# Stage 1 of a hybrid encoder kernel: x two tiles ahead, and another order of tables, value weights and value products

## The chip, the cores and the metric

The kernel runs on one core of a Trainium2 chip. The metric is the device time of one execution in microseconds (us). The engines are named as the profile names them: PE (TensorE, matmuls and transposes; its weight loads are PEld), DVE (VectorE), ACT (ScalarE), POOL (GpSimd) and SP (SyncE, which here only issues DMAs). Each engine takes its instructions in one fixed order.

## The reference

One encoder layer is applied to two groups of tokens (2048 and 512, model width 1024), with the same weights:

```python
xn = rms_norm(h, mix_norm)
z = xn @ w_in                      # 1024 x 2848
(a_q, a_k, a_v, a_gate, l_q, l_k, l_v, l_gate, lr_f, lr_b) = jnp.split(z, idx, axis=-1)
q = apply_axial_rope(rms_norm(a_q per head, q_norm), tables)
k = apply_axial_rope(rms_norm(a_k per head, k_norm), tables)
o_attn = block_attention(q, k, v)                   # 8 query heads, 2 key heads
o_gla = rms_norm(o_fwd + o_bwd, gla_norm)           # gated linear attention, both directions
h = h + concat[o_attn * silu(a_gate), o_gla * silu(l_gate)] @ w_out
gate = sigmoid(rms_norm(h, ple_norm) @ w_ple_gate)
return h + gate * (p @ w_ple_proj)                  # then a final rms_norm
```

## The kernel before

The work is staged: stage 1 (lines 111 to 343) normalises x and makes the projections that attention and the linear attention's values need; stage 2 is the linear attention, stage 3 the attention and the gates, stage 4 the output. Stages hand over through scratch tensors in HBM. Every fp32 matmul product is made from a high and a low part of both operands (`mm3`, line 101: three matmuls for each k of 128).

Stage 1 runs over 20 tiles of 128 tokens. For each tile `prep` loads the next x, takes the square sum on ACT, the power and the product `xn` on POOL (`x_r`, `xn`), transposes `xn` on PE (8 transposes into two PSUM tiles `pt`), copies the high part `xt` on ACT (line 203), makes the low part on DVE (line 204), and stores both. `project` makes three products of 24 matmuls each, into PSUM tiles `pm` (four banks): the queries with the weights `wq` (512 columns), keys, values and low-rank codes with `wm` (288), and the low-rank values with `wl` (512). After the first two come `rope` (square sums of the heads, the products with the cosine table `cqk` and the sine table `sqk`, into `rot` and `swp`), then on POOL the sum of the two, the power `h_r` of the heads' square sums and the product with it; that is called the rotation below. `post` transposes the result of the tile before and stores it. The xn tile has one buffer, x has two.

Ahead of the loop stand, in program order: 32 warm-up transposes of the identity, `prep(0)`, the weights `wq`, the load of x(1), the weights `wm` with the 32 low-rank columns `wlr`, the weights `wl`, the scale of the values (`value_scale`: squares, two small PE products, two powers on POOL), and the rope tables (loads of `ctab`, `stab` and of the head norms `qn`; two `cqk` products and eight `sqk` products, all on DVE). Each weight of 1024 rows is eight loads, eight casts on ACT (`*_h`, line 99) and eight differences on DVE (`*_l`, line 100). In the loop, tile t+1 is prepared before tile t is projected, and tile t-1 is posted after it:

```python
            nxt = prep(t + 1) if t + 1 < NT else None
            cur = project(t, xt)
            if pend is not None:
                post(t - 1, *pend)
            pend, xt = cur, nxt
```

The order in each engine's queue is not the program's. A scheduler writes it when the kernel is built: whenever an engine comes free in its own estimate of the run, it takes, of the instructions whose inputs and buffers it estimates to be ready, the first in program order. `high_priority(n)` ranks what is traced under it n places further ahead; `issue_after(e)` puts what is traced under it behind `e` on e's engine, without waiting for e to finish. Semaphores keep the run right whatever the estimate was; where the chip is late, the engine stands.

Of the kernel before, what the change touches and what calls it, by code (L numbers as in the profile page):

```python
# [9 lines left out]
F32 = mybir.dt.float32  # L10
F32R = mybir.dt.float32r
F16 = mybir.dt.float16
BF16 = mybir.dt.bfloat16
U32 = mybir.dt.uint32
AF = mybir.ActivationFunctionType
# [5 lines left out]
P = 128  # L21
# [30 lines left out]
class Net:  # L52
# [49 lines left out]
    def mm3(self, out, lh, ll, rh, rl, first=True, last=True):  # L102
        pairs = ((lh, rh), (ll, rh), (lh, rl))
        n = len(lh) * 3
        i = 0
        for k in range(len(lh)):
            for a, b in pairs:
                self.nc.tensor.matmul(out, lhsT=a[k], rhs=b[k], start=first and i == 0, stop=last and i == n - 1)  # L108
                i += 1


def stage1(net, s, gw=None):
    nc, tc, d = net.nc, net.tc, net.d
    with ExitStack() as ctx:
# [15 lines left out]
        def load_x(t):  # L130
            src = xs[0][t * P:(t + 1) * P] if t < 16 else xs[1][(t - 16) * P:(t - 15) * P]
            x = xp.tile([P, 1024], F32, name="x", tag="x")
            nc.sync.dma_start(out=x, in_=src)
            return x
# [37 lines left out]
        def part(w, c0, c1):  # L172
            return lambda k: w[:, k, c0:c1]
# [9 lines left out]
            for j in range(2):  # L183
                nc.sync.dma_start(out=s["wg"][i % 2][:, :, j, k].rearrange("j p e -> p j e"), in_=f(hl[:, j]))

        def prep(t):
            c, tt = t // 4, (t % 4) * P
            x = xq.pop(0)
            if 0 < t < NT - 1:
                xq.append(load_x(t + 1))  # L190
            ssq = net.sm.tile([P, 1], F32, name="x_ssq")
            xn = xp.tile([P, 1024], F32, name="xn", bufs=1)
            nc.scalar.activation(xn, x, AF.Square, accum_out=ssq)
            r = net.rstd(ssq, 1024.0, 1, "x")
            nc.gpsimd.tensor_scalar(xn, x, r, 1.0, ALU.mult, ALU.mult)
            xt = xp.tile([P, 2, 8, P], F32R, name="xt", bufs=2)
            for half in range(2):
                pt = ps_t.tile([P, 4, P], F32, name="pt")
                for k in range(4):
                    kk = half * 4 + k  # L200
                    nc.tensor.transpose(pt[:, k], xn[:, kk * P:(kk + 1) * P], net.ident)
                sl = slice(half * 4, half * 4 + 4)
                nc.scalar.copy(xt[:, 0, sl], pt)  # L203
                nc.vector.tensor_tensor(xt[:, 1, sl], pt, f(xt[:, 0, sl]), ALU.subtract)
            nc.sync.dma_start(out=s["xt"][c][:, :, :, tt:tt + P], in_=f(xt))
            return xt

        def project(t, xt):
# [3 lines left out]

            def proj(w, n):
                ps = ps_m.tile([P, 512], F32, name="pm")[:, :n]
                net.mm3(ps, lh, ll, [w[0][:, k] for k in range(8)], [w[1][:, k] for k in range(8)])
                return ps

            hs = net.sm.tile([P, 10], F32, name="hs")
# [30 lines left out]
            hr = net.rstd(hs, 64.0, 10, "h")  # L249
            nc.gpsimd.tensor_tensor(rot, rot, swp, ALU.add)  # L250
            nc.gpsimd.tensor_tensor(rot, rot, hr.unsqueeze(2).broadcast_to([P, 10, 64]), ALU.mult)
            pl = proj(wl, 512)
            lv = tp.tile([P, 512], F32, name="lv")
            nc.scalar.copy(lv, pl)
            nc.sync.dma_start(out=s["lv"][t // 4][t % 4], in_=lv)
            return rot.rearrange("p h e -> p (h e)"), lrin

        def post(t, rf, lrin):
            c, tt = t // 4, (t % 4) * P
# [18 lines left out]
            nc.sync.dma_start(out=s["lr"][c][:, tt:tt + P], in_=f(lr))  # L278

        warm = ps_q.tile([P, 4, P], F32, name="pqt")  # L280
        for i in range(32):
            nc.tensor.transpose(warm[:, i % 4], net.ident, net.ident)
        xt = prep(0)
        first = stage if gw is None else gw.stage
        net.weight(first, part(wq[0], 0, 512), part(wq[1], 0, 512), win, COL_Q, 512, mix)
        xq.append(load_x(1))
# [3 lines left out]
        nc.vector.tensor_tensor(w, w, mix.unsqueeze(2).broadcast_to([P, 8, 32]), ALU.mult)  # L290
        nc.scalar.copy(wm[0][:, :, 256:288], w)
        nc.vector.tensor_tensor(wm[1][:, :, 256:288], w, f(wm[0][:, :, 256:288]), ALU.subtract)
        net.weight(first, part(wl[0], 0, 512), part(wl[1], 0, 512), win, COL_LV, 512, mix)

        vscale = [value_scale()]

        ctab, stab = (gp.tile([P, 1024], F32, name=n, tag="wghl").rearrange("p (t e) -> p t e", t=16)
                      for n in ("ctab", "stab"))
        nc.sync.dma_start(out=ctab, in_=d["rope_c"])
# [19 lines left out]
        for w in range(2):  # L319
            nc.vector.tensor_tensor(cqk[:, :, w], ctab, qn[:, w:w + 1, :].broadcast_to([P, 16, 64]), ALU.mult)  # L320
            sv = sqk[:, :, w].rearrange("p t (a b e) -> p t a b e", a=2, b=2)
            tv = stab.rearrange("p t (a b e) -> p t a b e", a=2, b=2)
            for b in range(2):
                for a in range(2):
                    nc.vector.tensor_tensor(
                        sv[:, :, a, b], tv[:, :, a, b],
                        qns[:, w, a, 1 - b].unsqueeze(1).broadcast_to([P, 16, 16]), ALU.mult)

        pend = None
        for t in range(NT):  # L330
            if t >= 2 and t < 18:
                gate_weight(t - 2)
                if gw is not None and t % 2 == 0:
                    gw.main(stage, mix, t // 2 - 1, t // 2)
                if gw is not None and t == 17:
                    gw.small(tp)
            nxt = prep(t + 1) if t + 1 < NT else None
            cur = project(t, xt)
            if pend is not None:
                post(t - 1, *pend)  # L340
            pend, xt = cur, nxt
# [853 lines left out]
```

## Time and profile before

| | us |
|---|---|
| median of 3 runs | 2087.77 (2084.49 to 2088.56) |
| the profiled execution | 2088.21 |
| span of its trace | 2086.5 |
| PE busy | 2004.7 (96%) |
| DVE busy | 1332.6 (64%) |
| ACT busy | 1181.5 (57%) |
| POOL busy | 356.5 (17%) |

Stage 1 takes about the first 340 us of the span. PE's busy time says when a matmul was in it, not at which clock; the granted clock has a row of its own. The rows below come from the first 64 us of that execution and from one later tile; the POOL groups of rows 8 count the whole stage or execution. In rows that are listed in order of time, a group "x8" of equal instructions runs from the start given for the length given, and the brackets give how long the engine had been idle before it and what ended the wait.

### The profile page before, as it was taken

How to read it: one execution, taken by the hardware profiler on the slowest of the kernel's cores; microseconds unless marked ns; L12 is line 12 of the kernel's file. 1: busy time of each engine (PE TensorE's matmuls, PEld its weight loads, DVE VectorE, ACT ScalarE, POOL GpSimd, SP SyncE). 2: the span in 40 equal slices, each digit the busy share in tenths (PEclk: the TensorE clock that was granted, in tenths of full speed). 3: DMA queues.
4: the chain of work that ended last, by engine and by line, in shares of the span. 5: the costliest groups of instructions: out<-in, count | busy, mean ns of one | idle time of the engine just before them, and what ended most of it. 6: DMA issues, size and time to landing. Idle time of an engine off the chain costs nothing.

```text
span 2086.5 us, 29717 instructions
## 1 busy us (share of the span) xinstructions
PE 2004.7 (96%) x11174; PEld 1321.1 (63%) x11174; DVE 1332.6 (64%) x2242; ACT 1181.5 (57%) x2048; POOL 356.5 (17%) x292
## 2 busy tenths in 40 slices
PE   8999999999979999999999999999989999999998
PEld 7788887777754444444444444444437888888886
DVE  7555444665678889899889989988874222222223
ACT  5343233555558888788878878878883222222222
POOL 2434431000430011011011011100120111111111
PEclk9999999999999999999999999999999999999999
DMA  8887445666775225333333422522236222222220
GB/s 269 241 254 209 134 128 167 202 203 199 227 229 188 79 97 171 106 112 108 114 112 128 143 80 94 177 68 93 80 115 187 86 86 86 86 86 86 81 66 33
DMA packets 251360, 282.23 MB, mean 135 GB/s; under 512 B 41872, under 2 KB 180976, under 8 KB 246096
## 3 DMA queue, kind: packets, MB, share of 16 engines
q1 hardware_dynamic: 251072, 279.80, 43.0%
q8 instruction: 88, 1.44, 0.3%
q0 software_dynamic: 144, 0.52, 0.1%
q14 instruction: 56, 0.46, 0.1%
HBM read 189.64 MB, written 90.64 MB: 134 GB/s over the span
## 4 chain that ended last, share of the span: by engine, by line
PE 79%; DVE 8%; ACT 7%; DMA 3%; issue 2%; POOL 1%; SPq 0%; DVEq 0%; POOLq 0%; ACTq 0%
PE pm L108 38%; PE pg L728 9%; PE po L805 5%; PE px L762 4%; PE pss L816 4%; PE pss L817 4%; ACT p L818 3%; PE po L797 3%; PE pp L108 3%; PE pz L801 2%; DVE plo L827 2%; DVE mx L768 2%; ACT phi L825 2%; PE pn L845 1%; PE pt L1080 1%
## 5 line engine op out<-in xcount | busy, mean ns | idle before, releaser
L818 ACT ACTIVATE p<-pss,lnp,qk_scale 128x512 f32<-128x512 f32 x544 | 407.3, 781 | 113.4 <-PE pss L817 100.9
L768 DVE TENSOR_REDUCE mx<-px 128x1 f32<-128x512 f32 x544 | 357.0, 682 | 68.1 <-PE px L762 66.6
L728 PE MATMUL pg<-xt,wg 128*128 128x512 f32 x960 | 376.4, 484 | 1.1 <-DVE g L733 0.9
L827 DVE TENSOR_TENSOR plo<-p,phi 128x1024 f16<-128x1024 f32 x272 | 338.9, 1248 | 34.6 <-ACT phi L825 32.8
L825 ACT CAST phi<-p 128x1024 f16<-128x1024 f32 x270 | 283.2, 1049 | 5.6 <-PE po L805 0.9
L728 PEld LDWEIGHTS pg<-xt,wg 128*128 128x128 f32 x960 | 181.7, 190 | 69.1 <-issue 6.7
L816 PE MATMUL pss<-qa,ka 128*128 128x512 f16 x544 | 208.8, 385 | 11.1 <-ACT p L818 10.2
L762 PE MATMUL px<-ka,qa 128*128 128x512 f16 x544 | 201.0, 384 | 10.3 <-DVE mx L768 6.3
L817 PE MATMUL pss<-qb,kb 66*128 66x512 f16 x544 | 206.4, 383 | 0.3 <-ACT qb L781 0.3
L1128 DVE SCALAR_TENSOR_TENSOR th<-th,pp 128x512 f32<-128x512 f32 (+1 forms) x41 | 27.7, 675 | 190.0 <-ACT th L1127 190.0
L805 PE MATMUL po<-phi,v 128*128 128x512 f16 x544 | 142.5, 385 | 0.0
L108 PE MATMUL pm<-xt,wlqk 128*128 128x512 f32 x480 | 120.4, 410 | 7.8 <-DMA xt<-scr_xt 6.3
L816 PEld LDWEIGHTS <-ka 128*128 128x128 f16 x544 | 52.8, 97 | 107.0 <-issue 83.7
L1081 ACT CAST hT<-pt 128x512 fp32r<-128x512 f32 x40 | 23.5, 587 | 169.7 <-PE pt L1080 169.7
L108 PEld LDWEIGHTS pm<-xt,wlqk 128*128 128x128 f32 x480 | 94.3, 199 | 30.0 <-DMA xt<-scr_xt 7.5
L108 PE MATMUL pm<-wq_h,xt 128*128 128x512 f32 x320 | 103.2, 403 | 4.5 <-ACT xt L203 4.3
L762 PEld LDWEIGHTS <-qa 128*128 128x128 f16 x544 | 52.4, 98 | 83.9 <-issue 41.9
L1127 ACT ACTIVATE th<-pm,rh 128x512 f32<-128x512 f32 (+1 forms) x41 | 27.9, 680 | 133.8 <-PE pm L108 133.8
L108 PE MATMUL pm<-wpg0h,hT 128*128 128x512 f32 x320 | 101.0, 396 | 0.1
L108 PE MATMUL pm<-wo0h,mx 128*128 128x512 f32 x320 | 100.5, 395 | 0.0
L108 PE MATMUL pm<-wo1h,mx 128*128 128x512 f32 x320 | 100.4, 394 | 0.0
L851 POOL TENSOR_TENSOR ou<-ou,rs 128x512 f32<-128x512 f32 x20 | 35.5, 1777 | 378.5 <-DVE rs L849 378.5
(250 smaller groups left out, 3866.1 us busy)
## 6 DMA issues: line engine op xcount, KB each, us to landing
wg<-scr_wg SPq DMA_DIRECT2D x40, 1024.0 KB
scr_xt<-xt SPq DMA_DIRECT2D x20, 1024.0 KB
xt<-scr_xt SPq DMA_DIRECT2D x20, 1024.0 KB
xt<-scr_xt SPq DMA_DIRECT2D x40, 512.0 KB
scr_mx<-hl SPq DMA_DIRECT2D x40, 512.0 KB
mx<-scr_mx SPq DMA_DIRECT2D x20, 1024.0 KB
x<-x_prompt SPq DMA_DIRECT2D x27, 512.0 KB
scr_wg<-wghl SPq DMA_DIRECT2D x32, 256.0 KB
```

Of the source, the lines that this page charges most:

```text
L108: self.nc.tensor.matmul(out, lhsT=a[k], rhs=b[k], start=first and i == 0, stop=last and i == n - 1)
L728: nc.tensor.matmul(ps, lhsT=w[:, wi, k], rhs=xi, start=i == 0, stop=i == 23)
L762: nc.tensor.matmul(ps, lhsT=q[0][:, b * P:(b + 1) * P], rhs=ks[ti][0][:, h // 4], start=True, stop=True)
L768: nc.vector.tensor_reduce(mx[:, b, i:i + 1], product(i, b), axis=AX.X, op=ALU.max)
L797: nc.tensor.matmul(po[r:r + 32], lhsT=ks[t // 4][2][:, t % 4 + i, kv, g * 32:g * 32 + 32], rhs=lo[:, i], start=t == 2, stop=False)
L801: nc.tensor.matmul(pz[i * 32:i * 32 + 32], lhsT=ones, rhs=(lo, hi)[i // 2][:, i % 2], start=t == 2, stop=t + 4 == n)
L805: e = nc.tensor.matmul(po, lhsT=ks[t // 4][2][:, t % 4 + i, kv], rhs=hi[:, i], start=False, stop=t + i + 1 == n)
L816: nc.tensor.matmul(ps, lhsT=ka[:, kv, cs], rhs=q[0], start=True, stop=False)
L817: nc.tensor.matmul(ps, lhsT=kb[0:66, kv, cs], rhs=q[1][0:66], start=False, stop=True)
L818: e = nc.scalar.activation(p[:, i], ps, AF.Exp, bias=net.lnp, scale=net.qk_scale)
L825: nc.scalar.copy(hi, p)
L827: nc.vector.tensor_tensor(lo, p, hi, ALU.subtract)
```

## The change

- **x.** `prep` is cut in two. `norm(t)` takes x, its square sum (the square itself now goes to a bf16 tile of its own), the power and `xn`, and loads x(t+2); it is called two tiles ahead, and `xn` has two buffers. `prep(t, xn)` keeps the transposes, the copies and the store.
- **Start.** 40 warm-up transposes at rank 200; `prep(0)` at rank 100, its PE part behind the last warm-up.
- **Order.** The rope tables come before the weights `wl`, and x(2) is loaded between them. The eight `sqk` products move from DVE to POOL.
- **Products.** `project` stops before the value product. For tiles 0 and 1 the order of the products is q(0), k(0), preparation of tile 1 behind q(0)'s last matmul on PE, q(1), k(1), value(0), then preparation of tile 2, value(1). From tile 2 on the order in a tile is as before, with `norm(t + 2)` called between k and value.

```diff
         for k in range(len(lh)):
             for a, b in pairs:
-                self.nc.tensor.matmul(out, lhsT=a[k], rhs=b[k], start=first and i == 0, stop=last and i == n - 1)
+                e = self.nc.tensor.matmul(out, lhsT=a[k], rhs=b[k], start=first and i == 0, stop=last and i == n - 1)
                 i += 1
+        return e
...
-        def prep(t):
-            c, tt = t // 4, (t % 4) * P
+        def norm(t):
             x = xq.pop(0)
-            if 0 < t < NT - 1:
-                xq.append(load_x(t + 1))
             ssq = net.sm.tile([P, 1], F32, name="x_ssq")
-            xn = xp.tile([P, 1024], F32, name="xn", bufs=1)
-            nc.scalar.activation(xn, x, AF.Square, accum_out=ssq)
+            xn = xp.tile([P, 1024], F32, name="xn", bufs=2)
+            sq = xp.tile([P, 1024], BF16, name="xsq", bufs=1)
+            nc.scalar.activation(sq, x, AF.Square, accum_out=ssq)
             r = net.rstd(ssq, 1024.0, 1, "x")
             nc.gpsimd.tensor_scalar(xn, x, r, 1.0, ALU.mult, ALU.mult)
+            if 0 < t < NT - 2:
+                xq.append(load_x(t + 2))
+            return xn
+
+        def prep(t, xn):
+            c, tt = t // 4, (t % 4) * P
             xt = xp.tile([P, 2, 8, P], F32R, name="xt", bufs=2)
...
-                net.mm3(ps, lh, ll, [w[0][:, k] for k in range(8)], [w[1][:, k] for k in range(8)])
+                ends.append(net.mm3(ps, lh, ll, [w[0][:, k] for k in range(8)], [w[1][:, k] for k in range(8)]))
                 return ps
...
+            yield
             pl = proj(wl, 512)
             lv = tp.tile([P, 512], F32, name="lv")
             nc.scalar.copy(lv, pl)
             nc.sync.dma_start(out=s["lv"][t // 4][t % 4], in_=lv)
-            return rot.rearrange("p h e -> p (h e)"), lrin
+            yield rot.rearrange("p h e -> p (h e)"), lrin
...
         warm = ps_q.tile([P, 4, P], F32, name="pqt")
-        for i in range(32):
-            nc.tensor.transpose(warm[:, i % 4], net.ident, net.ident)
-        xt = prep(0)
+        with tc.high_priority(200):
+            for i in range(40):
+                e = nc.tensor.transpose(warm[:, i % 4], net.ident, net.ident)
+        xn = norm(0)
+        with tc.high_priority(100), tc.issue_after(e.ins):
+            xt = prep(0, xn)
...
-        net.weight(first, part(wl[0], 0, 512), part(wl[1], 0, 512), win, COL_LV, 512, mix)
-
         vscale = [value_scale()]
-
...
-                    nc.vector.tensor_tensor(
+                    nc.gpsimd.tensor_tensor(
                         sv[:, :, a, b], tv[:, :, a, b],
                         qns[:, w, a, 1 - b].unsqueeze(1).broadcast_to([P, 16, 16]), ALU.mult)
-
-        pend = None
+        xq.append(load_x(2))
+        net.weight(first, part(wl[0], 0, 512), part(wl[1], 0, 512), win, COL_LV, 512, mix)
+
+        pend, ends = None, []
+        xn = norm(1)
...
-            nxt = prep(t + 1) if t + 1 < NT else None
-            cur = project(t, xt)
+            if t == 0:
+                gen = project(0, xt)
+                next(gen)
+                with tc.issue_after(ends[0].ins):
+                    nxt = prep(1, xn)
+                early = project(1, nxt)
+                next(early)
+            else:
+                nxt = prep(t + 1, xn) if t + 1 < NT else None
+                gen = early if t == 1 else project(t, xt)
+                if t > 1:
+                    next(gen)
+            xn = norm(t + 2) if t + 2 < NT else None
+            cur = next(gen)
```

## Rows read from the trace of the kernel before

**Rows 1.** Busy time by engine in one tile's stretch; columns as in its head.

```profile
core 0: us, PE busy (x) PEld busy (x) DVE busy (x) ACT busy (x) POOL busy (x), PEclk, DMA share, GB/s
246.50:262.17 15.67, 15.67 (x87) 13.67 (x87) 7.19 (x19) 4.92 (x13) 6.48 (x5) 1.00 0.53 147
```

**Rows 2.** PE's waits to 420 us: for whom, us in total, times, longest.

```profile
PE pt L201 <- POOL xn L195: 6.8, 2, 4.7
PE pm L108 <- ACT xt L203: 4.3, 1, 4.3
```

**Rows 3.** PE in order of time: start us, length us, what [idle before, releaser].

```profile
1.43 5.53 PE L282 MATMUL pqt<-ident 128*128 128x128 f32 x32 [1.43 <-POOL ident masks.py:199]
...
14.41 0.79 PE L108 MATMUL pm<-wq_h,xt 128*128 128x512 f32 x1 [4.30 <-ACT xt L203]
...
29.61 0.63 PE L108 MATMUL pm<-wl_h,xt 128*128 128x512 f32 x2
...
35.10 0.61 PE L108 MATMUL pm<-wq_h,xt 128*128 128x512 f32 x2
...
40.54 0.42 PE L108 MATMUL pm<-wm_h,xt 128*128 128x288 f32 x2
...
46.05 1.03 PE L201 MATMUL pt<-ident,xn 128*128 128x128 f32 x8
46.84 0.48 PE L108 MATMUL pm<-wl_h,xt 128*128 128x512 f32 x1
...
56.57 1.97 PE L201 MATMUL pt<-ident,xn 128*128 128x128 f32 x8 [4.71 <-POOL xn L195]
...
63.59 0.42 PE L108 MATMUL pm<-wm_h,xt 128*128 128x288 f32 x2
```

**Rows 4.** Half microseconds, columns as in rows 1: the clock rises in them.

```profile
18.50:19.00 0.50, 0.50 (x3) 0.37 (x2) 0.32 (x2) 0.50 (x2) 0.33 (x1) 0.65 1.01 290
59.50:60.00 0.50, 0.50 (x3) 0.36 (x3) 0.39 (x1) 0.50 (x1) 0.00 (x0) 0.69 0.00 0
```

**Rows 5.** POOL in order of time.

```profile
40.52 1.57 POOL L250 TENSOR_TENSOR rot<-rot,swp 128x640 f32<-128x640 f32 x1 [5.88 <-DVE swp L233]
...
48.94 1.56 POOL L250 TENSOR_TENSOR rot<-rot,swp 128x640 f32<-128x640 f32 x1 [3.56 <-DVE swp L233]
50.61 2.40 POOL L80 TENSOR_TENSOR h_r<-h_ms,mhalf 128x10 f32<-128x10 f32 x1
...
55.40 1.12 POOL L195 TENSOR_SCALAR xn<-x,x_r 128x1024 f32<-128x1024 f32 x1
```

**Rows 6.** DVE in order of time.

```profile
18.76 0.42 DVE L292 TENSOR_TENSOR wm_l<-wlr,wm_h 128x256 fp32r<-128x256 f32 x1 [0.18 <-ACT wm_h L291]
...
27.03 4.06 DVE L100 SCALAR_TENSOR_TENSOR wl_l<-wst,mixn,wl_h 128x512 fp32r<-128x512 f32 x6
...
33.61 1.22 DVE L320 TENSOR_TENSOR cqk<-ctab,qn 128x1024 f32<-128x1024 f32 x1
...
37.30 1.42 DVE L325 TENSOR_TENSOR sqk<-stab,qn 128x256 f32<-128x256 f32 x4
...
39.24 0.74 DVE L233 TENSOR_TENSOR swp<-pm,sqk 128x256 f32<-128x256 f32 x2
```

**Rows 7.** ACT in order of time.

```profile
12.58 1.30 ACT L99 ACTIVATE wm_h<-wst,mixn 128x256 fp32r<-128x256 f32 x3 [0.96 <-DMA wst<-w_in]
13.79 1.05 ACT L203 CAST xt<-pt 128x512 fp32r<-128x512 f32 x2
...
31.96 0.30 ACT L306 ACTIVATE qabs<-qn 128x128 f32<-128x128 f32 x1
```

**Rows 8.** POOL's elementwise groups; mean ns of one behind the comma.

```profile
L250 POOL TENSOR_TENSOR rot<-rot,swp 128x640 f32<-128x640 f32 x20 | 31.3, 1567 | 98.9 <-DVE swp L233 78.3 <-DVE lrin L242 20.6
L851 POOL TENSOR_TENSOR ou<-ou,rs 128x512 f32<-128x512 f32 x20 | 35.5, 1777 | 378.5 <-DVE rs L849 378.5
```

**Rows 9.** SP's queue in order of time: the norms' load.

```profile
26.07 0.33 SPq L302 DMA_DIRECT2D qn<-q_norm  x1
```

## The prediction

> **What bounds the kernel now.** I read the list of TensorE's (PE's) waits first, then the stretches of single tiles, then the queues of each engine in time order over the first 75 us. The profiled execution took 2088.21 us, of which the trace spans 2086.5; the median of the runs is 2087.77. My sum is made against the first and lowered by their distance, 0.44 us.
>
> Stage 1 (to about 340 us) is bound by PE: one whole tile takes 15.67 us, and PE is busy for all of it [rows 1]. Twenty such tiles are the same work after the change, so only what PE loses at the start of stage 1 is in play. The waits show two losses: 6.8 us for POOL's `xn` in two waits, of which one is 4.7, and 4.3 us for ACT's `xt` [rows 2]. In PE's queue [rows 3] the first matmul starts at 14.41 after 4.30 us of waiting, and from 51.87 (the wait of 4.71 is in the row) nothing runs until 56.57.
>
> The granted clock adds to both. [...]
>
> **Why PE waits at 51.87.** It is the transposing of tile 3 that waits. POOL's queue [rows 5] shows tile 3's `xn` behind the head rotation of tile 1: `rot` at 48.94, the power for the head norms at 50.61 (2.40 us), then `xn` only at 55.40. Tile 1's rotation was late because DVE made the rope tables late: the low-rank value weights `wl_l` until 31.09, the first `cqk` product at 33.61, the last four `sqk` products until 38.72, and only then rope of tile 0 [rows 6].
>
> **The change, part by part.**
>
> *Normalising two tiles early.* `xn` of tile 3 is now asked for during tile 1's value product, a tile ahead of its transposes, and has its own second buffer. The 4.71 us of waiting (51.87 to 56.57 [rows 3]) go. With them goes the slow clock behind: from 56.57 to 63.59 PE does 8 transposes and 21 matmuls in 7.02 us. At full clock the transposes take 0.79 (46.05 to 46.84) and a matmul of this kind 0.227 (24 of them from 35.10 to 40.54 [rows 3]), so 0.79 + 4.77 = 5.56. That is 1.46 us more. What stands next in line is PE itself.
>
> *Norm work itself.* The square (now to a bf16 tile), the power and the product are the same instructions at the same count. The loads of x come one tile sooner on SP's queue and on the same buffers; x(2) becomes 0.5 MB ahead of the value weights. I cost these at nothing; PE's work on tiles 0 and 1 hides them.
>
> *Warm-up of 40, tile 0 ahead.* In ACT's queue the two `xt` copies of tile 0 stand behind three `wm_h` casts, which themselves waited for their loads until 12.58 [rows 7]. That is why PE waits 4.3 us. A higher rank decides only between instructions that the scheduler estimates to be ready; tile 0's preparation came ahead of all weights in program order before too, and lost its place all the same, so its estimated readiness was the reason. Eight more warm-up transposes ahead of it can only move that estimate back. Eight at 0.173 us (5.53 for 32 [rows 3]) are 1.4 us, at most three casts of 0.43 more; none, if the estimate hangs on `xn`. Between 14.41 and 15.7, then; I take two casts, a first matmul at 15.27. PE runs at half clock in that time, so 0.86 us late are 0.43 us of full-clock work. Cost: 0.4 us. The other end, copies right behind the transposes, is a rival below.
>
> *Tables ahead of the value weights; `sqk` to POOL.* DVE gives up 8 products of 0.36 us (2.84 for 8). No row has them on POOL. By POOL's 1567 ns for 128x640 one of 128x256 costs 0.63, by its 1777 ns for 128x512 0.89 [rows 8]: 5.0 to 7.1 us for 8. I take 0.63, whose row is in this stage, so 5.0. POOL had been idle for 5.88 us when the rotation of tile 0 began at 40.52 [rows 5], and the first user is rope of tile 0. [...]
>
> *New order of products.* Before, the four `pm` banks of PSUM held q(0), k(0), value(0), q(1), and k(1) at 40.54 needed the bank of q(0), which rope freed at 39.98 [rows 3, 6]. Now they hold q(0), k(0), q(1), k(1), and value(0) needs it. q(0), k(0) and the second preparation ended at 29.61 before [rows 3]; 0.43 later, plus 5.44 and 3.19 for q(1) and k(1), is 38.7. Is rope of tile 0 done by then? The norms' load `qn` is issued at 26.07, behind the value-scale chain [rows 9], and ACT took it up at 31.96 [rows 7]. From there it took 1.65 us to the first cosine product and 0.74 for the swap [rows 6]. With four or eight `sqk` ahead: 31.96 + 1.65 + 2.5 (or 5.0) + 0.74 = 36.9 to 39.4, and up to 4 us sooner if ACT takes `qn` up when it lands. Cost: zero, with ends of 0 and 2.8 us (eight at 0.89 give 41.5 against 38.7). The value weights' second halves take DVE 0.68 us apiece (6 in 4.06 [rows 6]), and value(0) uses one in 0.68 (three matmuls); with a start ahead of 38.7 they keep up. Cost: nothing.
>
> **Sum.** 4.71 + 1.46 - 0.43 = 5.7 us. 2088.21 - 5.7 = 2082.5; against the median 2082.0. Its own range is 2079.5 to 2083.5.
>
> **Rivals.**
>
> *1. The start moves forward.* If the copies of tile 0 stand right behind its transposes, the first matmul comes up to 4.30 us sooner. But k(0) needs the last part of `wm_l`, done at 19.18 [rows 6], and q(0) doesn't last that long; PE stands before k(0) and may lose its clock again. From 19.18 on it still has k(0) (3.19), tile 1 (15.67), value(0) (5.44) and some 2 us of small products: 45.5, or 47 with the loss of clock, against 50.7 for the same point before (three matmuls ahead of the wait). That is 3.7 to 5.2 on top of 4.71 + 1.46: 2078 to 2076.4, likeliest 2078. For it: the rank and the edge are aimed there. Against: the readiness argument.
>
> *2. value(0) waits for its bank.* As worked out, 1 to 2.8 us, or more if `qn` lands behind x(2) (0.5 MB at 290 GB/s is 1.8 [rows 4]): 2083.5 to 2086.5, likeliest 2085.
>
> *3. The change doesn't do what it says.* `xn` of tile 3 stays behind both rotations. If POOL ends `sqk` at 39.4, two tiles' POOL work (48.94 to 55.40 is 6.46 for one) and the `xn` (1.12 [rows 5]) end at 53.4, where PE wants it near 51; that is half of the old wait, and any DVE delay between brings back the rest. Against: `xn` of tile 3 has its input long before, and POOL is idle ahead of the tables. 2085 to 2088, likeliest 2087.
>
> *4. Slower: the value weights come late.* Their loads now stand behind the tables, x(2) and, at worst, behind two waits in SP's queue (the stores of `xt`, and `qn` [rows 9]). PE would stop before value(0) at 38.7, and every us counts, with about 1.5 for the clock from some 4 us on. It ends slower than before once the first cast comes after 43, and measurably so after 47. For that the loads would have to be issued after 40, behind tile 1's stores; nothing in the queue before points that far. 2090 to 2094.
>
> **How the numbers follow.** Forecast 0.50, rival 1 0.17, rival 2 0.16, rival 3 0.10, rival 4 0.07. The likeliest gives 2082. The range takes in rival 1 down to 2076 and rival 2 and most of rival 3 up to 2087.5. A measurement of this kernel tells about 0.2% (4.2 us) from no change; the forecast lies 1.6 us past that line, and the runs themselves spread by 4 us, so a fifth of it counts as no change. Faster: 0.40 + 0.17 + 0.04 = 0.61; slower 0.07 and a little for spread, 0.08; same 0.31.
>
> **What would show it.** In PE's waits the 4.7 us for `xn` must be gone, and no half clock between 20 us and the end of stage 1. ACT's `xt` copies of tile 0 behind three to six `wm_h` casts, first matmul at 14.4 to 15.7: right; copies before any `wm_h` cast: rival 1. A wait of `pm` for DVE's `swp` near 38: rival 2; for `wl_h` or `wl_l`: rival 4. The last matmul of stage 1 must come some 6 us sooner, and the stages behind must take what they took; if they do not, the sum has missed a place.

## The result: slower

| | before | after |
|---|---|---|
| median, us | 2086.03 (6 runs, 2084.49 to 2088.56) | 2096.97 (6 runs, 2093.67 to 2101.47) |
| profiled execution, us | 2088.21 | 2094.54 |
| its span, us | 2086.5 | 2092.8 |
| end of stage 1 in it, us | 340.18 | 353.22 |

Three more runs of the kernel before lower its median from 2087.77. The ratio is 1.0052, with an interval of 1.0037 to 1.0067: about 11 us slower, clear of noise though only half a per cent, where 2082.0 and a range of 2076.0 to 2087.5 were forecast. The end of stage 1 is read from the start of the last tile's transposes of `rot`, first in the kernel before, then in the changed one (start us, length us, what, idle before and its releaser):

```profile
340.18 0.63 PE L263 MATMUL pqt<-ident,rot 128*128 128x128 f32 x4 [1.32 <-DVE qt L268]
...
353.22 0.63 PE L269 MATMUL pqt<-ident,rot 128*128 128x128 f32 x4 [1.32 <-DVE qt L274]
```

So stage 1 takes 13.04 us more. PE's waits to 330 us in the changed kernel, the longest four (for whom: us in total, times, longest):

```profile
PE pm L108 <- DVE swp L238: 12.5, 1, 12.5
PE pm L108 <- ACT xt L208: 5.7, 2, 5.5
PE pt L206 <- POOL xn L194: 1.6, 1, 1.6
PE pm L108 <- DVE xt L209: 1.5, 2, 0.8
...
```

Against [rows 2]: `xn` gives back 5.2 us, 4.7 of them for tile 3, as was meant, and 0.5 for tile 0, whose transposes now come after a longer warm-up. The high half of `xt` costs 1.4 more, 1.15 for tile 0 (5.45 after 4.30) and the rest for tile 1; the low half, which had cost 0.2, costs 1.3 more. A new wait of 12.5 us for `swp` takes the place of everything gained. That is 10.0 us more. Of the other 3.0, 0.7 are the longer warm-up (6.21 us in PE's queue below, 5.53 before). The rest is mostly slow clock: PE's busy time at half clock (granted clock 0.50), counted half, comes to 5.9 us after and 3.7 before, 2.1 more; 0.2 us stay unexplained. Three stretches show the waits and the clock (length, PE busy and its matmuls, granted clock, DMA share, GB/s), first before, then after:

```profile
14.00:31.00 17.00, 16.02 (x88) 0.86 0.92 289
31.00:48.00 17.00, 17.00 (x90) 1.00 0.75 213
48.00:65.00 17.00, 12.29 (x60) 0.90 0.75 217
```

```profile
14.00:31.00 17.00, 14.25 (x74) 0.77 0.62 177
31.00:48.00 17.00, 3.78 (x16) 0.63 0.65 216
48.00:65.00 17.00, 16.68 (x78) 0.86 0.71 221
```

In the middle stretch PE has almost no work (3.78 us), and the clock falls to half: it is 0.50 from 36.0 to 52.5, and 1.00 again from 53.0. PE in order of time, to be held against [rows 3]:

```profile
1.43 6.21 PE L289 MATMUL pqt<-ident 128*128 128x128 f32 x40 [1.43 <-POOL ident masks.py:199]
...
15.77 0.79 PE L108 MATMUL pm<-wq_h,xt 128*128 128x512 f32 x1 [5.45 <-ACT xt L208]
...
31.06 1.03 PE L206 MATMUL pt<-ident,xn 128*128 128x128 f32 x8
32.37 0.50 PE L108 MATMUL pm<-wq_h,xt 128*128 128x512 f32 x1 [0.27 <-ACT xt L208]
32.71 0.29 PE L108 MATMUL pm<-wm_h,xt 128*128 128x288 f32 x1
45.51 1.19 PE L108 MATMUL pm<-wl_h,xt 128*128 128x512 f32 x2 [12.50 <-DVE swp L238]
...
48.32 0.80 PE L108 MATMUL pm<-wq_h,xt 128*128 128x512 f32 x1 [0.76 <-DVE xt L209]
```

q(0) and k(0) are followed by tile 1's transposes, by one matmul each of q(1) and k(1), and then, at 33.0, by the first matmul of value(0). It needs the bank of q(0), and rope of tile 0 frees that only at 45.4. Who holds it up stands in the queues of DVE, POOL, SP and ACT, one after the other ([rows 5, 6, 7, 9] show the same before):

```profile
32.84 1.77 DVE L326 TENSOR_TENSOR cqk<-ctab,qn 128x1024 f32<-128x1024 f32 x1
...
36.87 7.83 DVE L100 SCALAR_TENSOR_TENSOR wl_l<-wst,mixn,wl_h 128x512 fp32r<-128x512 f32 x8
44.62 0.74 DVE L238 TENSOR_TENSOR swp<-pm,sqk 128x256 f32<-128x256 f32 x2
...
47.59 0.68 DVE L209 TENSOR_TENSOR xt<-pt,xt 128x512 fp32r<-128x512 f32 x1
```

```profile
32.77 9.39 POOL L331 TENSOR_TENSOR sqk<-stab,qn 128x256 f32<-128x256 f32 x8 [7.01 <-DVE qn L319]
```

```profile
26.18 0.33 SPq L308 DMA_DIRECT2D qn<-q_norm  x1
...
27.50 5.50 SPq L97 DMA_DIRECT2D wst<-w_in  x8
```

```profile
31.37 0.31 ACT L312 ACTIVATE qabs<-qn 128x128 f32<-128x128 f32 x1 [2.56 <-DMA qn<-k_norm]
...
33.74 5.07 ACT L99 ACTIVATE wl_h<-wst,mixn 128x512 fp32r<-128x512 f32 x8
```

Read from SP on: the load of `qn` still goes out at 26.18, where [rows 9] had it at 26.07, since its buffer, shared with the tiles of the value-scale chain, waits for that chain. The eight loads of the value weights now stand behind it and go out from 27.50 to 33.0. Their first halves are cast on ACT until 38.8, their second halves fill DVE's queue from 36.87 to 44.70, and the swap of tile 0, which frees the bank, stands behind all eight. The low half of tile 1's `xt`, needed for q(1), comes later still. So PE has neither q(1) nor value(0).

### The profile page after: what moved, and what is told of

Its sections match the earlier page's. It is cut to its first block, busy times and chain, and to the rows that moved or that the text cites. A ratio compares the mean times of both kernels' runs of the same rounds, so it can differ in the third digit from the quotient of the medians.

```text
span 2092.8 us, 29710 instructions
## 1 busy us (share of the span) xinstructions
PE 2004.0 (96%) x11182; PEld 1322.1 (63%) x11182; DVE 1334.4 (64%) x2234; ACT 1180.4 (56%) x2048; POOL 365.2 (17%) x300
## 4 chain that ended last, share of the span: by engine, by line
PE 78%; DVE 8%; ACT 7%; DMA 3%; issue 3%; POOL 1%; SPq 0%; DVEq 0%; POOLq 0%; ACTq 0%
PE pm L108 38%; PE pg L749 8%; PE po L826 5%; PE px L783 4%; PE pss L837 4%; PE pss L838 4%; ACT p L839 3%; PE po L818 3%; PE pp L108 3%; DVE plo L848 2%; PE pz L822 2%; DVE mx L789 2%; ACT phi L846 2%; PE pn L866 1%; PE pt L1101 1%
## 5 line engine op out<-in xcount | busy, mean ns | idle before, releaser
L108 PE MATMUL pm<-xt,wlqk 128*128 128x512 f32 x480 | 115.6, 399 | 2.5 <-ACT l L474 1.7
L108 PE MATMUL pm<-wl_h,xt 128*128 128x512 f32 x320 | 100.1, 393 | 12.5 <-DVE swp L238 12.5
L783 PEld LDWEIGHTS <-qa 128*128 128x128 f16 x544 | 52.5, 98 | 83.6 <-issue 41.7
L872 POOL TENSOR_TENSOR ou<-ou,rs 128x512 f32<-128x512 f32 x20 | 35.5, 1775 | 378.6 <-DVE rs L870 378.6
```

The costliest lines, as they stand in the source:

```text
L108: e = self.nc.tensor.matmul(out, lhsT=a[k], rhs=b[k], start=first and i == 0, stop=last and i == n - 1)
L783: nc.tensor.matmul(ps, lhsT=q[0][:, b * P:(b + 1) * P], rhs=ks[ti][0][:, h // 4], start=True, stop=True)
```

## The experiments

Each timed kernel is given by its ratio to the kernel before on the same chip, with the interval. The theory: value(0) now hangs on rope of tile 0, which hangs on value weights that were put behind `qn`; the early norms themselves gain. (The letters A, B and C in the expectations are each run's own.) Its rivals: the products on POOL are the cause; the new order of products alone is the cause; or the whole change gains and stage 2 loses.

### Parts of the change undone

**Tile 1's preparation traced first.** The loop's edge goes, too:

```diff
-                gen = project(0, xt)
-                next(gen)
-                with tc.issue_after(ends[0].ins):
-                    nxt = prep(1, xn)
+                nxt = prep(1, xn)
+                gen = project(0, xt)
+                next(gen)
```

> The changed kernel, with the preparation of tile 1 traced ahead of q(0) again (no edge behind q(0)). Theory A (the moved preparation): in the changed kernel DVE makes the low half of tile 1's xt only at 47.6 to 49.1, behind the eight wl_l and rope of tile 0, so PE has no q(1) and k(1) to do while it waits 12.5 us for the bank of q(0). Here PE does them first (8.6 us), the wait for swp falls from 12.5 to about 4, the last matmul of stage 1 comes 8 to 10 us sooner, and the time is 2086 to 2090. Theory B (the sqk products on POOL are the cause): the bank comes free at the same time, near 45; the wait falls by the same 8.6, so the same time. Theory C (the loss is the value product's place): the wait stays above 8 us, 2093 to 2097.

Measured: 2089.28 us median of 12, ratio 1.0008 [0.9992, 1.0023]. Stage 1 ends at 348.21, 5.0 us sooner than in the changed kernel, and PE's wait for `swp` falls to 5.12 us, at 49.24:

```profile
49.24 1.19 PE L108 MATMUL pm<-wl_h,xt 128*128 128x512 f32 x2 [5.12 <-DVE swp L238]
```

PE has q(1) and k(1) to do meanwhile; value(0) still comes too early for rope. Stage 1 was expected to end 8 to 10 us sooner. In the one profiled execution the first half clock lasted until 29.75 instead of 22.0 (two `wq_h` matmuls took 1.05 us before and 0.62 behind it), which cost PE 3.7 us more; the ratio of the runs is the better measure of what this edit brings. Theories A and B had forecast the same here, so this run does not choose between them.

**The sine products back on DVE.**

```diff
-                    nc.gpsimd.tensor_tensor(
+                    nc.vector.tensor_tensor(
                         sv[:, :, a, b], tv[:, :, a, b],
```

> The changed kernel with the eight sqk products on DVE again. Theory A: DVE makes them in 2.9 us instead of POOL's 9.4, but the eight wl_l still stand ahead of rope of tile 0 in DVE's queue, and the low half of tile 1's xt behind both; the wait for q(0)'s bank stays at 11 to 14 us: 2094 to 2099. Theory B (POOL's 9.4 us are what ends last): sqk is done near 38 instead of 42.2, the wait falls by about 4 us to 8: 2089 to 2093. Theory C: as A.

Measured: 2095.57, ratio 1.0037 [1.0025, 1.0049]; the wait for `swp` is 11.5 us where it was 12.5. POOL is not the cause of the 12.5: the swap stands behind the value weights' halves on DVE either way.

```profile
36.74 5.38 DVE L100 SCALAR_TENSOR_TENSOR wl_l<-wst,mixn,wl_h 128x512 fp32r<-128x512 f32 x8
...
42.65 0.74 DVE L238 TENSOR_TENSOR swp<-pm,sqk 128x256 f32<-128x256 f32 x2
```

**The old order of products.** The branch for tile 0 goes, and each tile is projected whole:

```diff
-            if t == 0:
-                ...
+            nxt = prep(t + 1, xn) if t + 1 < NT else None
+            gen = project(t, xt)
+            next(gen)
```

> The changed kernel with the order of products of the kernel before: preparation of tile 1, then q(0), k(0), value(0), q(1), k(1), value(1). No product waits for q(0)'s bank before k(1). Theory A: most of the loss goes, but value(0) now comes at about 31 and has to wait for wl_l, which DVE makes from 36.9 on at 0.98 us each, while some of q(1) lies between: a wait of 3 to 6 us for wl instead of 12.5 for swp: 2087 to 2092. Theory B: rope of tile 0 stays late, k(1) waits for the bank: 2092 to 2097. Theory C: the whole loss goes and the forecast gain comes: 2080 to 2083.

Measured: 2094.51, ratio 1.0032 [1.002, 1.0044]. The wait for `swp` is gone, but stage 1 still ends at 352.23:

```profile
PE pm L108 <- ACT xt L208: 5.8, 1, 5.8
PE pt L206 <- POOL xn L194: 4.7, 2, 3.7
PE pm L108 <- ACT wl_h L99: 2.7, 1, 2.7
PE pm L108 <- DVE wl_l L100: 1.6, 1, 1.6
```

PE now waits for the value weights themselves (4.3 us, theory A's range), and their lateness carries rope and `xn` back again. The time lies in theory B's range all the same. In this execution PE stands 6.0 us less than in the changed kernel, but has about 5 us more of slow clock, 3.7 of them in the first half clock (until 29.75 here too), so stage 1's end tells little of the order. That with late value weights the old order loses too is shown below, where the tables are moved with the old start.

**The value weights ahead of the tables again.**

```diff
+        net.weight(first, part(wl[0], 0, 512), part(wl[1], 0, 512), win, COL_LV, 512, mix)
         vscale = [value_scale()]
...
         xq.append(load_x(2))
-        net.weight(first, part(wl[0], 0, 512), part(wl[1], 0, 512), win, COL_LV, 512, mix)
```

> The changed kernel, but with the value weights loaded and cast ahead of the rope tables again, as in the kernel before; the rest of the change stays. Theory (the value weights behind the tables are the other half of the loss, beside the new order of products): the casts of the value weights are over by about 31 us on DVE, so the second half of tile 1's xt no longer stands behind eight of them and rope of tile 0 follows the tables directly; TensorE's wait for swp falls from 12.5 us to some 2 (the sine products on POOL end at about 42, q(1) and k(1) at 40), and the time is near 2086 us (2083 to 2089). Rival (the order of products alone makes the loss, the place of the value weights none): the wait for swp stays above 8 us and the time at 2093 to 2097.

Measured: 2086.49, ratio 0.9992 [0.9978, 1.0006]. The wait for `swp` falls to 1.4 us, for POOL's last products, and the loss is gone with this one move:

```profile
45.83 0.71 PE L108 MATMUL pm<-wl_h,xt 128*128 128x512 f32 x2 [1.37 <-DVE swp L238]
```

The gain of the early norms is not seen yet. The profiled execution (2090.05, 3.6 above the median) has half clock until 29.75 (a mean of 0.54 from 14 to 31 us) and a wait of 2.4 us for `xn`, and its stage 1 ends at 345.32, 7.9 us sooner than in the changed kernel and 5.1 later than before.

### Parts of the change alone

**Normalising two tiles early, nothing else** (two buffers for `xn`, `norm` two tiles ahead, the square to bf16). It was run in two sets:

```diff
-            xn = xp.tile([P, 1024], F32, name="xn", bufs=1)
+            xn = xp.tile([P, 1024], F32, name="xn", bufs=2)
...
+            xn = norm(t + 2) if t + 2 < NT else None
```

> The kernel before with the first part of the change alone: x loaded and normalised two tiles early, bf16 square, two xn buffers; 32 warm-ups without ranks, value weights ahead of the tables, sqk on DVE, old order of products. By the first term of the prediction's sum the wait of 4.7 us for tile 3's xn and the slow clock behind it go: 6.2 us less than the kernel before, about 2080. If the normalising was not what PE waited for in the end (rival 3), the wait comes back elsewhere: within 2 us of the kernel before.

> The kernel that only normalises two tiles early once more, as the base of the three others on the same chip. Theory: ratio 0.9963 to 0.9983 to the kernel before, as it was; 2079 to 2084. Rival (that result was a lucky set of runs, since one kernel's runs spread by up to 15 us): 2084 to 2088, no difference from before.

Measured: 2082.44, 0.9973 [0.9963, 0.9983], and again 2082.52, 0.9986 [0.9977, 0.9995]: faster both times, by 0.2% on average; the second ratio lies just outside the 0.9963 to 0.9983 expected of it. A wait for `xn` of 2.8 us is left in both. It is that of tile 2: its `xn` stands on POOL behind the rotation of tile 0, which hangs on the tables.

The four others add one part each to this kernel (0.998, the mean of its two ratios).

**The tables ahead of the value weights.**

```diff
-        net.weight(first, part(wl[0], 0, 512), part(wl[1], 0, 512), win, COL_LV, 512, mix)
         vscale = [value_scale()]
...
         xq.append(load_x(2))
+        net.weight(first, part(wl[0], 0, 512), part(wl[1], 0, 512), win, COL_LV, 512, mix)
```

> The kernel before with two parts of the change alone: normalising two tiles early, and the rope tables ahead of the value weights (sine products on DVE, 32 warm-up transposes, the old order of products). It differs from the kernel that only normalises early (2082.4) in the place of the tables alone. Theory (the loads of the value weights now stand behind two waits of SP's queue, and their casts come too late for value(0)): first cast of wl_h after 31 us where it was 19 before, TensorE waits 3 to 8 us for wl_h, wl_l or xt between 30 and 45 us, and the time is 2086 to 2091. Rival (tables early cost nothing as long as value(0) comes at its old place, since q(1) fills in): 2081 to 2084, no wait above 3 us for the value weights.

Measured: 2089.85, 1.002 [1.0007, 1.0033], 0.41% above its base. The time is the theory's, the wait for the value weights a little under its 3 us. PE stands before value(0) until ACT casts the first value weights, and then for `xn` of tile 2:

```profile
32.91 1.22 PE L108 MATMUL pm<-wl_h,xt 128*128 128x512 f32 x2 [2.78 <-ACT wl_h L99]
...
51.16 1.97 PE L206 MATMUL pt<-ident,xn 128*128 128x128 f32 x8 [3.85 <-POOL xn L194]
```

**The sine products on POOL.** The edit of the second experiment, the other way round.

> The kernel before with normalising two tiles early and the sine products on POOL, nothing else of the change. It differs from the kernel that only normalises early (2082.4) in the engine of the eight products alone. Theory (1.17 us apiece on POOL, 9.4 us in all, end at about 42 where DVE's ended at 39; rope of tile 0 is late by 2 to 3 us, and k(1) asks for its bank): TensorE waits 1 to 3 us for swp, xn of tile 3 waits as much as in the other or up to 3 us more; 2083 to 2087. Rival (POOL has the room; DVE's 2.8 us are a gain): 2080 to 2082.5, no wait for swp. Second rival (POOL's rotations of tiles 0 and 1 move back by the whole 9 us and with them xn of tile 3): 2088 to 2092.

Measured: 2086.77, 1.0002 [0.9985, 1.0018], 0.22% above its base; its interval overlaps with that of the base's second set. There is no wait for `swp`. PE's wait for `xn` of tile 2 is 6.30 us instead of 2.8, and yet POOL makes it no later:

```profile
36.62 7.68 POOL L330 TENSOR_TENSOR sqk<-stab,qn 128x256 f32<-128x256 f32 x8 [2.40 <-DVE qn L318]
44.64 1.54 POOL L255 TENSOR_TENSOR rot<-rot,swp 128x640 f32<-128x640 f32 x1 [0.34 <-DVE swp L238]
...
48.45 2.21 POOL L194 TENSOR_SCALAR xn<-x,x_r 128x1024 f32<-128x1024 f32 x2
```

In the base the rotation starts at 44.57 and `xn` at 48.81, so the 7.68 us of products are hidden there. What differs in the trace is PE's queue: the scheduler put tile 2's transposes ahead of value(1), where the base has them halfway through it, and PE asks at 43.3 instead of 47.2. The size was the theory's, the way was none of the three. The profiled execution is the fastest of the 12 (2081.55), and its stage 1 ends 2.2 us later than the base's; where the median loses its 4 us is not shown.

**The new order of products**, with value weights first and the sine products on DVE: the branch for tile 0 as in the change.

> The kernel before with normalising two tiles early, and the new order of products (q and k of tiles 0 and 1 ahead of the first value product), with the value weights ahead of the tables and the sine products on DVE as before. It differs from the kernel that only normalises early (2082.4) in the order of products alone. Theory (value(0) asks for the bank of q(0) at about 40, and rope of tile 0 frees it only after the tables, whose swap ended at 44.2 in that kernel): TensorE waits 3 to 5 us for swp, some slow clock behind it, 2085 to 2089. Rival (the order is harmless as long as the value weights come first): no wait above 1.5 us, 2081 to 2083.5.

Measured: 2085.75, 0.9994 [0.9984, 1.0005], 0.14% above its base; the interval overlaps with that of the base's second set. The wait that the prediction's second rival named is there, 3.0 us:

```profile
42.93 0.69 PE L108 MATMUL pm<-wl_h,xt 128*128 128x512 f32 x2 [3.00 <-DVE swp L238]
```

It takes the place of the 2.8 us for `xn`; stage 1 ends 1.7 us later.

**The new start.**

```diff
-        for i in range(32):
-            e = nc.tensor.transpose(warm[:, i % 4], net.ident, net.ident)
+        with tc.high_priority(200):
+            for i in range(40):
+                e = nc.tensor.transpose(warm[:, i % 4], net.ident, net.ident)
         xn = norm(0)
-        xt = prep(0, xn)
+        with tc.high_priority(100), tc.issue_after(e.ins):
+            xt = prep(0, xn)
```

> The kernel before with normalising two tiles early, and the changed start (40 warm-up transposes, rank and edge for tile 0). It differs from the kernel that only normalises early (2082.4) in the start alone. Theory (two more casts of wm_h stand ahead of the xt copies, and the slow clock costs by how long it lasts: it was half until 18.8 in two kernels with the old start, until 21.2 in one, and until 21.8 to 29.8 in three with the new one): first matmul at 15.3 to 16.1 where it was 14.6, half clock past 21, 2083.5 to 2087. Rival (the prediction's price: 0.86 us later at half clock, 0.4 us): 2082 to 2083.

Measured: 2078.81, 0.9966 [0.9953, 0.9979]. Theory and rival both missed: it is the fastest kernel of all, 3.7 us below its base on the same chip; with 5 runs against 9 the two intervals just touch. Its first matmul does come later (15.39 against 14.76), and value(0) starts 0.85 us later (30.86 against 30.01). But in ACT's queue `qabs` now comes ahead of the copy of value(0), and the tables start 3.3 us sooner. ACT and DVE in this kernel:

```profile
32.89 0.31 ACT L313 ACTIVATE qabs<-qn 128x128 f32<-128x128 f32 x1 [0.88 <-DMA qn<-k_norm]
...
36.55 0.59 ACT L260 COPY lv<-pm 128x512 f32<-128x512 f32 x1 [3.35 <-PE pm L108]
```

```profile
34.36 1.22 DVE L327 TENSOR_TENSOR cqk<-ctab,qn 128x1024 f32<-128x1024 f32 x1
```

and in its base:

```profile
35.70 0.59 ACT L260 COPY lv<-pm 128x512 f32<-128x512 f32 x1 [3.09 <-PE pm L108]
36.18 0.31 ACT L311 ACTIVATE qabs<-qn 128x128 f32<-128x128 f32 x1
```

```profile
37.66 1.22 DVE L325 TENSOR_TENSOR cqk<-ctab,qn 128x1024 f32<-128x1024 f32 x1
```

With that `xn` of tile 2 is in time: from 26 to 335 us the list of PE's waits is empty, and the granted clock is 1.00 from 31 to 97 us and 0.99 from there to 340. Stage 1 ends at 335.30, 3.5 us before its base and 4.9 before the kernel before. The gain is a by-product, as the queues show it: after the start was changed, `qabs` and the copy stand the other way round on ACT. No run moved `qabs` alone, so that this is what gains, and that the scheduler's shifted estimates did it, is argued and not shown; about 1 us of stage 1's 3.5 is a shorter first half clock (1.8 us of loss against 2.8).

**A try: `qn` in the place of `swp`, loaded ahead of the value weights.**

```diff
-        qn = tp.tile([P, 2, 64], F32, name="qn", tag="sq")
+        qn = tp.tile([P, 2, 64], F32, name="qn", tag="swp", bufs=1)
```

> A try at a better kernel: normalising two tiles early alone, and qn in the place of swp instead of one that waits for the value-scale chain, loaded and made ready ahead of the value weights. In the kernel that only normalises early DVE stood idle for 3.4 us before the tables (qabs on ACT came behind the copy of value(0)), and xn of tile 2 was late by 2.8 us behind rope of tile 0. Theory (the tables' delay is what holds xn): DVE starts the tables 3 us sooner, the wait of 2.8 us goes, 2078 to 2081. Rival (something else holds xn on POOL, or TensorE's start costs more as the value weights' loads move behind the first store of xt): 2082 to 2085.

Measured: 2081.9, 0.9983 [0.9972, 0.9993]: no better than its base. The tables start 4 us sooner (33.69), but the scheduler also moved tile 2's transposes ahead in PE's queue, and 2.1 us of the wait stay.

### Do the later stages give the loss back?

In the profiled executions the changed kernel lost 13.04 us in stage 1 and 6.3 in all. To see whether a later stage 1 is partly hidden, the kernel before was given 57 matmuls more in tile 10:

```diff
+                if t == 10 and n == 512:
+                    net.mm3(ps, lh, ll, [w[0][:, k] for k in range(8)], [w[1][:, k] for k in range(8)])
+                if t == 10 and w is wq:
+                    net.mm3(ps, lh[:3], ll[:3], [w[0][:, k] for k in range(3)], [w[1][:, k] for k in range(3)])
```

> The kernel before, with 57 matmuls more in tile 10 of stage 1 (products repeated into the same bank before they are made for good; the output is unchanged). At 0.227 us apiece stage 1 ends 12.9 us later than before (near 353, as in the changed kernel), by work in its middle and with no wait at its start. Theory (a part of a later end is given back in stage 2, where two waits of 3.5 and 2.8 us for the last quarter of xt and the slow clock behind them go): the time grows by less than the 12.9, by 8 to 11 us: 2096 to 2099. Rival (nothing is given back, and the changed kernel's 10.9 us come from a stage 1 that was later by only as much in most runs): 2100.5 to 2101.5.

Measured: 2102.61 median of 6, ratio 1.0067 [1.0048, 1.0085], 10 to 18 us more, with the end of stage 1 at 353.28, 13.1 us later. Nothing is seen to come back. The fourteen traces say the same. Behind the end of stage 1 their spans still have from 1738.8 to 1747.8 us to go, with no relation to how late that end is: 1747.8 in this kernel and 1739.6 in the changed one, whose stage 1 ends at the same time (353.28 and 353.22), 1746.3 in the kernel before (340.18) and 1739.7 in the second set of the early norms (338.83). Of the 6.7 us between the kernel before and the changed one, 5.5 are stage 2's waits for the loads of `xt`, 6.3 us before and 0.8 after; these too go up and down without regard to stage 1 (0.4 with an end at 335.30, 4.8 with 353.28). So the 6.3 us between the two profiled executions understate the loss by the spread of the later stages, and that the median rises by 10.9 us and not by 13 lies within the spread of the runs (8 us).

### The parts added up

Ratio above (or below) the base of 0.998: tables +0.0041, POOL +0.0022, products +0.0014, start -0.0014. They add up to 1.0043 for the changed kernel, which has 1.0052 [1.0037, 1.0067]. The tables' part is the largest loss, and the only one of the four whose interval lies apart from both of the base's. Taken out of the whole change it brings 0.0060, and tracing tile 1's preparation first 0.0044; both intervals lie apart from the changed kernel's. The old order of products brings 0.0020 and DVE for POOL 0.0015, with intervals that overlap with it. The two large ones do not add: each breaks the same chain, in which the late halves hold up both rope of tile 0 and tile 1's `xt`. That the sum comes so near is therefore worth little.

## Why the prediction was wrong

**The early norms: right.** The wait of 4.71 us at 51.87 and the slow clock behind it are gone. Where that part was alone, 2.8 us were then lost at the next wait of the same path, tile 2's `xn`; the prediction had said that PE itself stands next. With that wait gone too (the kernel with the new start, which holds just the parts that the sum priced), 6.8 us were gained on the median [0.9953, 0.9979], where 4.71 + 1.46 - 0.43 = 5.7 were worked out. That agreement is partly luck: the sum knew nothing of tile 2's `xn`, and it came in time by a change of places on ACT that nobody had planned.

**The start: right direction, too small.** Four `wm_h` casts stand ahead of the `xt` copies where there were three, and tile 1's square (1.06 us) before them. The first matmul comes at 15.77, past the bound of 15.7. Eight more warm-ups took 0.68 us and not 1.4. The price was 0.4 us, at half clock; the granted clock there was 0.50 from 12.5 to 18.5 before and to 21.5 after. Where the start was alone, value(0) came 0.85 us later. Two things were not foreseen. The order of `qabs` and the copy on ACT differs after the shift, which seems to be worth more than the shift. And the first half clock lasted until 29.75 in three of the six kernels with the new start (tile 1's preparation first, the old order, the value weights first); in the other three it ended at 20.0 to 22.0, and in the eight with the old start at 18.5 to 21.5. Counted as above it cost PE 6.4 to 6.8 us in the three and 1.7 to 3.2 in all others. With one trace of each kernel, whether the start causes it stays open.

**"`sqk` to POOL" at nothing: wrong in size and in cover.** The bounds were 5.0 to 7.1 us; the eight took 9.39 in the changed kernel, 7.68 and 6.75 in two others. The cover on POOL held where the part was alone: the rotation of tile 0 started 0.07 us later. The longer wait there came by PE's queue; in the whole change there is a price on DVE, whose value halves took 7.83 us beside POOL's products and 5.38 without them. The 0.63 and 0.89 apiece were the author's estimates from other shapes. In the changed kernel the quickest single product took 0.73 us on POOL and the slowest 1.79; the eight together, beside DVE's work, took 0.84 to 1.19 us apiece in the five kernels that had them there, 2.4 to 3.3 times as long as DVE's 2.84 for eight.

**"New order of products" at nothing: the upper end was right.** Its bounds were 0 and 2.8 us; 3.0 were measured where it was alone. The choice of zero rested on rope being done by 36.9 to 39.4, and so on the tables starting right after `qn`; they started at 36.41 with that order, behind `qabs` on ACT and the value weights' halves.

**"The value weights keep up, cost: nothing": the step that failed.** The prediction asked whether the halves are made as fast as value(0) uses them, "with a start ahead of 38.7". That condition was met: their loads went out from 27.50, right behind `qn`, whose 26.07 in [rows 9] gives that time already, and the first cast came at 33.74. What was put at nothing without a reason is what the eight halves do to others on DVE. Six of them had lain from 27.03 to 31.09 [rows 6], ahead of the tables. Now all eight, 7.83 us of work (5.38 without POOL beside it), stand in the one stretch where rope of tile 0 and tile 1's `xt` are urgent. In place of no cost the runs showed a wait of 12.5 us for `swp`. With the value weights ahead again it was 1.4 us and the ratio 0.9992 instead of 1.0052, and the tables' place alone cost 0.41%. The second rival (the bank, a wait of 1 to 2.8 us) and the fourth (late value weights, 2 to 6 us above the kernel before) were priced apart. They are one chain, since the late halves hold the very instruction that frees the bank. The sign that appeared was the second rival's, at more than four times its price; the fourth's test, a first cast after 43, was not met.

**When value(0) is asked for.** The prediction put q(1) and k(1) ahead of it in full (38.7). In the trace it is asked for at 33.0, as the low half of tile 1's `xt` was ranked behind the value weights' halves and the scheduler set value(0) ahead of q(1). An order in the program was taken for an order in the queue. Where tile 1's preparation was traced first, value(0) was asked for at 44.12, and the ratio was 1.0008 instead of 1.0052: without this second link the late halves cost much less.

## What to carry over

When a block of loads is moved behind another one, take the time of the last wait in front of it in the DMA queue as its earliest start (`qn` went out at 26.18, the value weights behind it from 27.50), and follow its work onto each engine that handles it: what becomes late there need not be the block itself; here it was what stands behind it. Price two rivals that meet in one queue as one chain. Where a kernel's order is a scheduler's, try each part of a change alone: here of five parts one gained as meant, the tables' place took more than that gave, and the other three are too small for these runs to price one by one.

## What the runs showed of the hardware

**POOL's products and DVE's work beside them.** The same product on POOL took a mean of 1207, 990 and 886 ns in three kernels (the changed one, POOL alone, value weights first):

```profile
L331 POOL TENSOR_TENSOR sqk<-stab,qn 128x256 f32<-128x256 f32 x8 | 9.4, 1207 | 7.0 <-DVE qn L319 7.0
```

```profile
L330 POOL TENSOR_TENSOR sqk<-stab,qn 128x256 f32<-128x256 f32 x8 | 7.7, 990 | 2.4 <-DVE qn L318 2.4
```

```profile
L332 POOL TENSOR_TENSOR sqk<-stab,qn 128x256 f32<-128x256 f32 x8 | 6.7, 886 | 0.0
```

In two more kernels, with the tables first as in the changed one (tile 1's preparation first, the old order of products), the eight took 9.48 and 9.46 us, where they took 9.39, 7.68 and 6.75 in these three. In the changed kernel the first `cqk` on DVE took 1.77 us instead of 1.22 beside it, the second 1.21; between them `qk_scale`, a product of one column, took 0.68 where it had taken 0.15, first before, then after:

```profile
34.75 0.15 DVE L315 TENSOR_TENSOR qk_scale<-big 128x1 f32<-128x1 f32 x1
...
34.52 0.68 DVE L321 TENSOR_TENSOR qk_scale<-big 128x1 f32<-128x1 f32 x1
```

The eight value halves took 7.83 us beside it and 5.38 where only the products' engine was changed. The slowest cases are those in which DVE ran `cqk` and the halves at the same time (1.17 to 1.19 us apiece); in the fastest (0.84) DVE ran the end of one `cqk`, the other and rope beside it, and stood idle for 2.9 us. No experiment here changed the inputs alone, so which part of DVE's work makes the difference is not shown.

**The clock isn't told by PE's busy time.** From 14 to 31 us PE was busy for 14.96 of 17 us in the kernel with the value weights first and for 14.48 in the one with the tables first, with granted clocks of 0.54 and 0.86 (columns as in the stretches above):

```profile
14.00:31.00 17.00, 14.96 (x53) 0.54 0.84 263
```

```profile
14.00:31.00 17.00, 14.48 (x82) 0.86 0.72 213
```

Nor did the clock fall after one length of gap, such as the 4 us of the prediction's fourth rival. In the kernel before nothing ran on PE from 51.87, and the clock was 1.00 until 56.0 and 0.90 in the half microsecond behind; in the changed kernel nothing ran from 33.0, and it was 1.00 until 35.5 and 0.53 in the half microsecond behind.

**The spread goes with the clock.** The times of one kernel lay up to 16 us apart, and they go with its mean granted clock: with the sine products on POOL alone, 12 runs went from 2081.55 at 0.988 to 2096.02 at 0.984, with a correlation of -0.94 (-0.64 to -0.96 in the sets of the other edited kernels, -0.71 to -0.81 in three of the kernel before). Which of the two leads isn't shown, since the clock was also half where PE had to wait, as in the 12.5 us for `swp`. A single profiled time of such a kernel says little about 5 us.
